# Row normalisation with each row written twice: the first load of each group as two transfers, gamma as two transfers and one broadcast

## The chip, the cores and the metric

The kernel runs on one core of one Trainium2 chip. The metric is the device time of one execution in microseconds (us). The kernel before was timed in three runs: 238.24, 238.38 and 238.87 us, so the median is 238.38. One execution was also taken with the hardware profiler. All views below are of that one.

## What is computed

```python
B, S, D = 8, 512, 2048          # x: [8, 512, 2048] float32, gamma: [2048] float32
x_rep = np.repeat(x, 2, axis=1)
rms = np.sqrt((x_rep ** 2).mean(axis=-1, keepdims=True) + 1e-6)
x_norm = x_rep / rms
return (x_norm * gamma[None, None, :]).astype(np.float32)
```

Each of the 4096 rows of x is divided by the root of its mean square, multiplied by gamma, and written twice, next to each other. So 33.55 MB are read and 67.11 MB are written.

## The kernel before

The 4096 rows go to 128 partitions in four tiles. In one tile each partition holds 8 rows that follow one another in memory, 64 KB. One large buffer `y` holds 24 rows of 2048 floats on each partition, in three regions of 8 rows: `first` (rows 0 to 7), `second` (8 to 15) and `third` (16 to 23). There are no rotating buffers: the regions are reused by hand, and the order of the instructions on each engine is the order of the program (a manual schedule). The waits between engines are put in by the framework, from who writes and reads which part of `y`.

`four(n, ...)` (L89) works on a group of two tiles, n and n+1, and is called twice. In one group:

- L92 loads the tile n to rows 4 to 11 of `y`, the upper half of `first` and the lower half of `second`. L94 loads the tile n+1 to `third`. Both are issued by SyncE (SP), one transfer each (L50).
- `squares` (L57) runs on ScalarE (ACT): for each row a Square with an accumulated sum (L63, its scratch output `sq` in PSUM), then one Sqrt for the group of rows (L67).
- `scale` (L70) runs on VectorE (DVE): the reciprocal (L73), and for each row one operation that multiplies the row by it and by gamma (L75), and writes the result to an even row of the region that is to be stored.
- `repeat` (L80) copies each even row to the odd row behind it (L82), on ACT or on DVE.
- `store` (L52) sends one region, 8 rows of each partition, to the output. There are four stores in a group, in this order: tile n's rows 0 to 3 from `first`, its rows 4 to 7 from `second`, and tile n+1's two halves from `first` again and from `third`.

The rows 0 to 3 of tile n are squared and scaled two by two, those from row 4 on four by four. All loads and stores are issued by SP, in program order: two loads, four stores, two loads, four stores. The loads of the second group write to rows that the first group's stores read, so SP waits for those stores to land before it issues them.

gamma is needed on every partition, in `gamma_b`. `constants()` (L121) is called between the two loads of the first group. ACT issues one transfer of 16 pieces of 125 floats (L122) and three of 16 floats each (L128) into rows 0 to 2 of `y` on partition 0, which the first store doesn't need yet. Then GpSimd (POOL) broadcasts first 2000 columns (L132) and then the last 48 (L136) to all partitions. A constant `eps_t` is set on DVE, and ACT takes one Sqrt of it (L140), which loads ACT's function table ahead of the work.

Of the kernel before, what the change touches and what calls it, by code (L numbers as in the profile page):

```python
# [1 line left out]

# [4 lines left out]


@with_exitstack
def kernel(  # L10
    ctx: ExitStack,
    tc: tile.TileContext,
    x: bass.AP,
    gamma: bass.AP,
    out: bass.AP,
):
    nc = tc.nc
    P = nc.NUM_PARTITIONS
    f32 = mybir.dt.float32
    Act = mybir.ActivationFunctionType  # L20
    Alu = mybir.AluOpType

    B, S, D = x.shape
    Bo, So, Do = out.shape
    R = So // S
    assert R == 2 and D == Do and B == Bo and So == S * R
    eps = 1e-6
    inv_d = 1.0 / float(D)


    K = 4
    N = B * S
    ntiles = N // (P * K)
    assert N % (P * K) == 0 and ntiles == 8
    H = 2
    x_t = x.rearrange("b s d -> (b s) d").rearrange("(n p k) d -> n p k d", p=P, k=H * K)
    out_t = out.rearrange("b s d -> (b s) d").rearrange("(n p h j) d -> n h p (j d)", p=P, h=H, j=K * R)

    singles = ctx.enter_context(tc.tile_pool(name="singles", bufs=1))
    rows = ctx.enter_context(tc.tile_pool(name="rows", bufs=1))  # L40
    junk = ctx.enter_context(tc.tile_pool(name="junk", bufs=1, space=bass.MemoryType.PSUM))
    small = ctx.enter_context(tc.tile_pool(name="small", bufs=4))

    y = rows.tile([P, 3 * K * R, D], f32, name="y")
    first, second, third = 0, K * R, 2 * K * R

    def load(n, at):
        nc.sync.dma_start(out=y[:, at : at + H * K, :], in_=x_t[n])  # L50

    def store(n, h, to):  # L52
        nc.sync.dma_start(
            out=out_t[n, h], in_=y[:, to : to + K * R, :].rearrange("p j d -> p (j d)")
        )

    def squares(at, rows):  # L57

        n = len(rows)
        ss = small.tile([P, n], f32, name=f"ss{n}")  # L60
        for c, k in enumerate(rows):
            sq = junk.tile([P, D], f32, name="sq")
            nc.scalar.activation(  # L63
                out=sq[:], in_=y[:, at + k, :], func=Act.Square, accum_out=ss[:, c : c + 1]
            )
        rms = small.tile([P, n], f32, name=f"rms{n}")
        nc.scalar.activation(out=rms[:], in_=ss[:], func=Act.Sqrt, scale=inv_d, bias=eps_t[:])  # L67
        return rms

    def scale(at, to, rows, rms):  # L70
        n = len(rows)
        rstd = small.tile([P, n], f32, name=f"rstd{n}")
        nc.vector.reciprocal(out=rstd[:], in_=rms[:])  # L73
        for c, k in enumerate(rows):
            nc.vector.scalar_tensor_tensor(  # L75
                out=y[:, to + R * k, :], in0=y[:, at + k, :], scalar=rstd[:, c : c + 1],
                in1=gamma_b[:], op0=Alu.mult, op1=Alu.mult,
            )

    def repeat(to, k0, k1, copy):  # L80
        y_r = y[:, to + R * k0 : to + R * k1, :].rearrange("p (k r) d -> p k r d", r=R)
        copy(out=y_r[:, :, 1, :], in_=y_r[:, :, 0, :])  # L82

    ctx.enter_context(tc.manual_schedule())

    half = K // 2
    up, down = list(range(K)), list(range(K - 1, -1, -1))

    def four(n, constants, step):  # L89


        load(n, first + K)  # L92
        constants()
        load(n + 1, third)  # L94
        for rows in (up[:half], up[half:]):
            scale(first + K, first, rows, squares(first + K, rows))
        repeat(first, 0, half, nc.scalar.copy)
        repeat(first, half, K, nc.vector.tensor_copy)
        store(n, 0, first)
        scale(second, second, down, squares(second, down))  # L100
        repeat(second, half, K, nc.scalar.copy)
        for k in range(0, half, step):
            repeat(second, k, k + step, nc.vector.tensor_copy)
        store(n, 1, second)
        roots = [squares(third + h * K, up) for h in range(H)]
        scale(third, first, up, roots[0])
        repeat(first, 0, half, nc.scalar.copy)
        repeat(first, half, K, nc.scalar.copy)
        store(n + 1, 0, first)
        scale(third + K, third, up, roots[1])  # L110
        repeat(third, 0, K, nc.scalar.copy)
        store(n + 1, 1, third)

    gamma_b = singles.tile([P, D], f32, name="gamma_b")
    G, E = 16, 3
    C = D // G - E
    gamma_s = y[0:1, 0:2, :].rearrange("p k (c d) -> p (k c) d", c=G // 2)
    gamma_t = y[0:1, 2, :]
    eps_t = singles.tile([P, 1], f32, name="eps_t")

    def constants():  # L121
        nc.scalar.dma_start(  # L122
            out=gamma_s[0:1, :, :C],
            in_=gamma[: G * C].rearrange("(p c d) -> p c d", p=1, c=G),
        )
        for c in range(E):
            at = G * C + c * G
            nc.scalar.dma_start(  # L128
                out=gamma_t[0:1, c * G : (c + 1) * G],
                in_=gamma[at : at + G].partition_broadcast(1),  # L130
            )
        nc.gpsimd.partition_broadcast(  # L132
            out_ap=gamma_b[:, : G * C].rearrange("p (c d) -> p c d", c=G),
            in_ap=gamma_s[0:1, :, :C],
        )
        nc.gpsimd.partition_broadcast(out_ap=gamma_b[:, G * C :], in_ap=gamma_t[0:1, : E * G])  # L136
        nc.vector.memset(eps_t, eps)  # L137

        root = singles.tile([P, 1], f32, name="root")[:]
        nc.scalar.activation(out=root, in_=eps_t[:], func=Act.Sqrt)  # L140

    four(0, constants, half)
    four(2, lambda: None, 1)


# [1 line left out]
_INS = ['x', 'gamma']  # L147
_OUTS = [((8, 1024, 2048), 'float32')]


# [23 lines left out]
```

## Time and profile before

| What | Value |
|---|---|
| median of three runs | 238.38 us (238.24 to 238.87) |
| profiled execution: its own time | 238.07 us |
| profiled execution: span from first to last instruction | 236.2 us |
| L63, Square on ACT, 32 times | 1.878 us each, 60.1 us in all |
| L75, scale on DVE, 32 times | 2.349 us each, 73.8 us in all |
| L82, copies on ACT / on DVE | 42.6 us in 10 / 9.2 us in 5 |
| first load of the first group: issued, and time to landing | 0.72 us, 21.9 us |
| first store of the first group / of the second: issued | 39.20 us / 155.30 us |

The span starts with the first instruction and ends with the last. Start times in all views are counted from it. In a view of waits, a line names an engine and a line of the program, what it waited for, the total, the number of times, and the longest. In a timeline, a line has the start, the duration, the engine, the line and the operation, and in brackets the idle time before it and what ended that. The name of an engine with a q behind it (SPq, ACTq) is its sequencer, which issues transfers. q1 is the DMA queue of SP and q10 that of ACT. Each transfer over 128 partitions is cut into packets, shared out over 16 DMA engines.

A DMA share over 1.00 in a short stretch comes about because a packet's whole time is put to the stretch in which it starts. So the share times the length of the stretch, times 16 engines, divided by the packets, is the mean time of a packet. "Packet records" are the starts and durations of single packets in the trace.

### The profile page before, as it was taken

What the parts mean: (1) busy time and instruction counts of PE and PEld (TensorE: products, weight loads), DVE (VectorE), ACT (ScalarE), POOL (GpSimd) and SP (SyncE); (2) the same over time, 40 slices, a digit from 0 to 9 for tenths busy, and PEclk for the clock granted to TensorE, in tenths of its full rate; (3) what the DMA queues carried; (4) which work ended last, traced back from release to release, by engine and by line L of the source; (5) the groups of instructions that cost most, each with busy time, mean ns of one, the idle gap of its engine ahead of it and who ended that gap; (6) DMA issues with size and microseconds to landing.
All of it is one profiled execution on the core that took longest, in us unless ns stands there. A gap on an engine that the chain in (4) does not pass through costs nothing.

```text
span 236.2 us, 226 instructions
## 1 busy us (share of the span) xinstructions
DVE 84.5 (36%) x48; ACT 110.2 (47%) x86; POOL 2.8 (1%) x6
## 2 busy tenths in 40 slices
DVE  0000396594699500000000007928919992000000
ACT  2001989479998470000000049991999957400000
POOL 0110000000000000000000000000000000000000
DMA  9898989989898989989898998989898998989894
GB/s 355 356 533 355 510 377 422 466 366 522 355 533 356 533 355 422 466 377 510 355 533 355 488 400 355 533 355 533 355 533 355 488 399 355 533 355 533 355 533 178
DMA packets 1767, 100.68 MB, mean 426 GB/s; under 512 B 230, under 2 KB 230, under 8 KB 230
## 3 DMA queue, kind: packets, MB, share of 16 engines
q1 hardware_dynamic: 1728, 100.66, 98.7%
q10 hardware_dynamic: 38, 0.01, 0.0%
q14 instruction: 1, 0.01, 0.0%
HBM read 33.56 MB, written 67.11 MB: 426 GB/s over the span
## 4 chain that ended last, share of the span: by engine, by line
DMA 45%; ACT 26%; DVE 12%; issue 2%; DVEq 0%
DMA y<-in_x_dram 26%; DMA out_dram<-y 20%; ACT sq L63 15%; DVE y L75 12%; ACT y L82 11%; ACT rms L67 1%; DVE rstd L73 0%; DVEq L75 0%
## 5 line engine op out<-in xcount | busy, mean ns | idle before, releaser
L63 ACT ACTIVATE sq<-y 128x2048 f32<-128x2048 f32 x32 | 60.1, 1878 | 71.1 <-DMA y<-in_x_dram 70.4
L75 DVE SCALAR_TENSOR_TENSOR y<-y,rstd,gamma_b 128x2048 f32<-128x2048 f32 x32 | 73.8, 2349 | 1.6 <-DMA out_dram<-y 1.0
L82 ACT COPY y<-y 128x4096 f32<-128x4096 f32 (+1 forms) x10 | 42.6, 4283 | 19.1 <-DVE y L75 18.3
L73 DVE RECIPROCAL rstd<-rms 128x4 f32<-128x4 f32 (+1 forms) x10 | 1.7, 170 | 109.2 <-ACT rms L67 109.2
L82 DVE COPY y<-y 128x4096 f32<-128x4096 f32 (+1 forms) x5 | 9.2, 1865 | 0.1
L63 ACT ACTIVATION_READ_ACCUMULATOR sq<-y 128x1 f32 x32 | 6.0, 186 | 0.0
L67 ACT ACTIVATE rms<-ss,eps_t 128x4 f32<-128x4 f32 (+1 forms) x10 | 3.0, 297 | 0.3
L140 ACT ACT_TABLE_LOAD x1 | 1.3, 1283 | 2.6 <-issue 2.6
L132 POOL PARTITION_BROADCAST gamma_b<-y x1 | 2.2, 2243 | 10.2 <-DMA y<-in_gamma_dram 10.2
L136 POOL PARTITION_BROADCAST gamma_b<-y x1 | 0.3, 323 | 10.1 <-DMA y<-in_gamma_dram 10.1
L137 DVE MEMSET eps_t<- 128x1 f32 x1 | 0.1, 59 | 0.8 <-PEq L158 0.8
L140 ACT ACTIVATE root<-eps_t 128x1 f32<-128x1 f32 x1 | 0.2, 203 | 0.0
L158 POOL MEMSET const-bfloat16-1.0<- 128x1 bf16 x1 | 0.1, 102 | 0.0
L158 POOL MEMSET const-float32-0.0<- 128x1 f32 x1 | 0.1, 99 | 0.2 <-issue 0.2
L158 POOL MEMSET const-uint8-127<- 128x1 uint8 x1 | 0.1, 101 | 0.0
L158 POOL MEMSET const-float32-1.0<- 128x1 f32 x1 | 0.1, 98 | 0.0
## 6 DMA issues: line engine op xcount, KB each, us to landing
out_dram<-y SPq DMA_DIRECT2D x8, 24.8
y<-in_x_dram SPq DMA_DIRECT2D x4, 31.4
y<-in_gamma_dram ACTq DMA_DIRECT2D x3, 0.1 KB
y<-in_gamma_dram ACTq DMA_DIRECT2D x1, 7.8 KB, 9.8
```

What stands on the lines that cost most here:

```text
L63: nc.scalar.activation(out=sq[:], in_=y[:, at + k, :], func=Act.Square, accum_out=ss[:, c : c + 1])
L67: nc.scalar.activation(out=rms[:], in_=ss[:], func=Act.Sqrt, scale=inv_d, bias=eps_t[:])
L73: nc.vector.reciprocal(out=rstd[:], in_=rms[:])
L75: nc.vector.scalar_tensor_tensor(out=y[:, to + R * k, :], in0=y[:, at + k, :], scalar=rstd[:, c : c + 1], in1=gamma_b[:], op0=Alu.mult, op ...
L82: copy(out=y_r[:, :, 1, :], in_=y_r[:, :, 0, :])
L132: nc.gpsimd.partition_broadcast(out_ap=gamma_b[:, : G * C].rearrange("p (c d) -> p c d", c=G), in_ap=gamma_s[0:1, :, :C],)
L136: nc.gpsimd.partition_broadcast(out_ap=gamma_b[:, G * C :], in_ap=gamma_t[0:1, : E * G])
L137: nc.vector.memset(eps_t, eps)
L140: nc.scalar.activation(out=root, in_=eps_t[:], func=Act.Sqrt)
L158: nc = _bacc.Bacc("TRN2", target_bir_lowering=False, num_devices=1)
```

## The change

Two parts. The first load of each group, in `four`, is issued as two transfers: rows 0 to 3 of each partition, then rows 4 to 7. The second load of a group stays one transfer. And gamma goes straight to partition 0 of `gamma_b`, in two transfers of 16 pieces of 64 floats (each takes one half of each stretch of 128 floats), and one broadcast of all 2048 columns from partition 0 of `gamma_b` to `gamma_b`. Rows 0 to 2 of `y` are no longer used for gamma.

```diff
-    def load(n, at):
-        nc.sync.dma_start(out=y[:, at : at + H * K, :], in_=x_t[n])
+    def load(n, at, parts=1):
+        w = H * K // parts
+        for k in range(0, H * K, w):
+            nc.sync.dma_start(out=y[:, at + k : at + k + w, :], in_=x_t[n][:, k : k + w, :])
...
-        load(n, first + K)
+        load(n, first + K, H)
         constants()
         load(n + 1, third)
...
-    G, E = 16, 3
-    C = D // G - E
-    gamma_s = y[0:1, 0:2, :].rearrange("p k (c d) -> p (k c) d", c=G // 2)
-    gamma_t = y[0:1, 2, :]
...
-        nc.scalar.dma_start(
-            out=gamma_s[0:1, :, :C],
-            in_=gamma[: G * C].rearrange("(p c d) -> p c d", p=1, c=G),
-        )
-        for c in range(E):
-            at = G * C + c * G
-            nc.scalar.dma_start(
-                out=gamma_t[0:1, c * G : (c + 1) * G],
-                in_=gamma[at : at + G].partition_broadcast(1),
-            )
-        nc.gpsimd.partition_broadcast(
-            out_ap=gamma_b[:, : G * C].rearrange("p (c d) -> p c d", c=G),
-            in_ap=gamma_s[0:1, :, :C],
-        )
-        nc.gpsimd.partition_broadcast(out_ap=gamma_b[:, G * C :], in_ap=gamma_t[0:1, : E * G])
+        G, E = 16, 2
+        w = D // G // E
+        g_in = gamma.rearrange("(p c d) -> p c d", p=1, c=G)
+        g_to = gamma_b[0:1, :].rearrange("p (c d) -> p c d", c=G)
+        for c in range(0, D // G, w):
+            nc.scalar.dma_start(out=g_to[:, :, c : c + w], in_=g_in[:, :, c : c + w])
+        nc.gpsimd.partition_broadcast(out_ap=gamma_b[:], in_ap=gamma_b[0:1, :])
         nc.vector.memset(eps_t, eps)
```

## The prediction

> **What bounds the kernel now.** I read the page's busy shares, then the DMA queues, then the share of the DMA engines in stretches of time, then the waits, and last the timeline around the two loads that the change splits.
>
> ```profile
> DVE 84.5 (36%) x48; ACT 110.2 (47%) x86; POOL 2.8 (1%) x6
> ...
> q1 hardware_dynamic: 1728, 100.66, 98.7%
> q10 hardware_dynamic: 38, 0.01, 0.0%
> ```
>
> No compute engine is busy for half of the span, while the 16 DMA engines spend 98.7% of it on q1, the queue of the x loads and the stores. What matters is where the missing 1.3% lies. Here are three stretches (start:end, length, busy time of DVE, ACT and POOL, clock, DMA share, GB/s):
>
> ```profile
> 0.00:1.70 1.70, 0.06 (x1) 0.00 (x0) 0.19 (x4) 1.00 0.00 0
> 1.70:235.05 233.35, 84.44 (x47) 110.16 (x86) 2.57 (x2) 1.00 1.00 431
> 235.05:236.20 1.15, 0.00 (x0) 0.00 (x0) 0.00 (x0) 1.00 0.00 0
> ```
>
> Between 1.70 and 235.05 the share is 1.00. The idle time is 1.70 us before the first packet (the first load is issued at 0.72 us) and 1.15 us after the last. So the transfers alone set the end, and a change can move it only by (a) making the transfers take more or less engine time, (b) moving the first packet or the tail, or (c) opening a hole in the stream.
>
> The waits seem to say something else:
>
> ```profile
> ACT sq L63 <- DMA y<-in_x_dram: 70.4, 2, 51.8
> ...
> SPq L53 <- DVE y L82: 84.1, 4, 35.2
> SPq L53 <- ACT y L82: 60.9, 4, 19.9
> ```
>
> ScalarE waits 70.4 us for loads, and the store queue waits for compute. But while those queues wait, the DMA engines work off what was issued before. The place to check is where loads run out and the first store must follow:
>
> ```profile
> 22.67 1.88 ACT L63 ACTIVATE sq<-y 128x2048 f32<-128x2048 f32 x1 [18.58 <-DMA y<-in_x_dram]
> ...
> 39.20 48.22 SPq L53 DMA_DIRECT2D out_dram<-y  x4
> ...
> 155.30 48.29 SPq L53 DMA_DIRECT2D out_dram<-y  x4
> ```
>
> Squares start at 22.67, when the whole first load has landed, and the first store is issued at 39.20. The DMA queue view for 36 to 46 us has q1 at 99.9%, so the loads reach past 41 us and the store follows without a hole. From issue to first packet the first load took 1.70-0.72 = 0.98 us, so the store was ready at about 40.2, some 0.8 us before the first engine came free at about 41.0 (packet records). In the second half it is ready at 156.3, against 157.3. The cover is thin but it holds.
>
> **The change, part by part.**
>
> *The first load of each group in two halves.* 100.66 MB in 12 transfers is 8.39 MB each, 19.5 us at 431 GB/s. A half lands 9.7 us earlier, so squares start near 13.0 instead of 22.67 and the store's chain, 39.20-22.67 = 16.5 us long, issues it near 29.5. What that saves is nothing: at 29.5 the engines still hold 11.5 us of loads, and the store waits behind them in its queue. The second group is alike: its first load, issued at 100.04, waits for the third store's landing as before, and the fourth store, in flight until about 119, hides that wait and SP's extra issue (0.36 us, from the row of L50). Later stores don't move the end either; the third needs a buffer that the first store frees near 61 us, whatever was computed before.
>
> What the halves add on the engines: 128 packets of 64 KB become 256 of 32 KB, 8 more on each engine, and one completion packet, per split load. The trace has no 32 KB packet, so I bound one packet's fixed part by the small ones, the two phases of the large gamma transfer on q10:
>
> ```profile
> q1 hardware_dynamic: 16, 1.05, 242.3%
> q10 hardware_dynamic: 16, 0.01, 2.6%
> ...
> ```
> ```profile
> q1 hardware_dynamic: 16, 1.05, 302.3%
> q10 hardware_dynamic: 16, 0.00, 1.1%
> ...
> ```
>
> The first pair is the stretch 7 to 8 us: 16 pieces of 500 B took 2.6% of 16 engine-us, 0.026 us each. The second is 9.5 to 10.3: 16 completion packets took 1.1% of 12.8, 0.009 us each, beside 64 KB packets of 302.3% x 12.8 / 16 = 2.418 us, or 27.1 B/ns. The 500 B at that rate are 0.018 us, which leaves 0.008 as the fixed part. Low end: nothing (bytes alone count; a gain is excluded, since the bytes stay and packets are only added). High end: the whole 0.026 for each added packet. I take 0.008, because a 32 KB packet streams as the large ones do. Sum for two loads: 2 x (8 x 0.008 + 0.009) = 0.15 us; high end 2 x (8 x 0.026 + 0.009) = 0.43 us. None of it is hidden, since the engines have no spare time.
>
> The rule that speaks against the split is in the Trainium skill, DMA: Bandwidth & Descriptors, "Anatomy of one DMA": a transfer costs a constant of about 2.0 us beside its bytes (fitted for transfers that GpSimd issues). By it, two added loads would make an estimated 238.07+4.0 = 242.1 us. The row of 36 to 46 us disagrees for queued transfers: one transfer ends and the next begins within it, and 99.9% of the engines' time is taken.
>
> *Gamma.* ACT issues two transfers instead of four (0.59 and 1.21 us of issue in the trace, in the 18 us in which ACT has nothing to square). On the engines, each had 0.026+0.009, and one had three small pairs more; now each has two pairs, at most 0.070 in all. The difference is below 0.04 us either way and I take 0. A wait could matter: the first scale now needs both transfers and a broadcast of all 2048 columns about 9.7 us sooner, at 27.34-9.7 = 17.6.
>
> ```profile
> 10.65 2.24 POOL L132 PARTITION_BROADCAST gamma_b<-y  x1 [10.22 <-DMA y<-in_gamma_dram]
> ...
> 23.01 0.32 POOL L136 PARTITION_BROADCAST gamma_b<-y  x1 [10.12 <-DMA y<-in_gamma_dram]
> ```
>
> Each q10 packet waits for one x packet of its engine: pieces at 7 to 8, completions at 9.5 to 10.3, and the three small pairs, six more turns, until 23.0. In the changed kernel the second transfer needs two turns more: 10.3 + 2 x 2.45 = 15.2, and the broadcast 2.24 x 2048/2000 = 2.3, so 17.5 at the latest; turns behind 32 KB packets are half as long, which gives nearer 10. If gamma came as late as 23.0, the broadcast would end at 25.3, DVE and the copies and store queued behind it would slip 7.7 us to 37.2, and that is still before 40. So cost 0, hidden by the loads; beyond 10.5 us of delay it would cost microsecond for microsecond. POOL has nothing else to do.
>
> *The new order of waits.* In the compiled order, SP's second store waits for the second half-load too, landed by 22, and the second half-load of group two also waits for the second store, landed near 80 before the 100 at which it is issued. Nothing behind them is late.
>
> *Sum.* The profiled execution: 238.07 (1.70 + 233.35 + 1.15, and 1.87 around the span) + 0.15 = 238.22. It lies 0.31 under the median of the three runs, 238.38, so for a median I forecast 238.38 + 0.15 = **238.5 us**.
>
> **Rivals.**
>
> *Slower: each added load opens the stream anew.* The queue view of 1.7 to 2.3 us has 16 packets with 537.3% of 16 x 0.6 engine-us, 3.22 us each, 0.81 over the usual 2.418. If a transfer of half the size pays that opening, two do: 238.5 + 1.6 = 240.1. It decides (over 0.72 us) from 0.28 us a load on, next to the 0.15. Against it: the boundaries between transfers in the trace show no such packets. For it: no row shows 32 KB packets or two loads from interleaved rows.
>
> *Faster: the thin cover had holes, or the stream's slow packets go.* The timed median is 0.31 over the profiled run and the slowest 0.80; if that were holes before the stores, 10 us of cover would close them: 238.07+0.15 = 238.2, still no change by my bound, and from the slowest run's level at best -0.65. To gain more, the opening's 0.81 and the slow packets near 116 us (323.4% x 12.8 / 16 = 2.59 each in 115.8 to 116.6, 0.17 over) must go as well: 238.2-1.0 = 237.2. Nothing in the change touches what makes them.
>
> *Compute was the bound after all.* If the 9.7 us by which compute moves forward reached the end in both groups, the time would be 238.4-19.4 = 219.0. A share of 1.00 over 233.35 us excludes it.
>
> *The halves don't land apart.* If the two half-loads ran interleaved, squares would start near 22 as now, and the time would be the same 238.5. Against it: the same queue's transfers land one after another, 19.3 us apart.
>
> **How the numbers follow.** A measurement of this kernel tells a change from none at about 0.3%, 0.72 us: the three runs spread over 0.63. No change 0.71 (the forecast with its costs, and the halves that don't land apart); slower 0.19 (the opening of loads, and other fixed costs above 0.04 us a packet); faster 0.10, nearly all of it the holes and slow packets, as the compute rival has next to nothing. The range: up to the slowest of the three runs plus the high end, 238.87+0.43 = 239.3; down to 237.7, the point where the faster case begins, which leaves out about a tenth on either side.
>
> **What would show it.** Right: squares start near 13, the first store is issued near 29.5 and lands, as before, near 61; q1 has 1728 + 2 x 144 = 2016 packets and a share of 1.00 from the first packet to the last; a stretch in the first load shows 32 KB packets of about 1.21 us. Wrong: those packets above 1.25 us, a stretch with a share under 1.00 at 12, 41, 129 or 158 us, or a first packet later than 1.7 us.

## The result and the profile after

The changed kernel takes 239.62 us (median of 6 runs, 239.31 to 239.96), the kernel before in the same comparison 238.39 us (238.24 to 238.87). The ratio is 1.0049, with a 95% interval of 1.0036 to 1.0062. So it is slower by 1.2 us, above the range of the prediction.

The profiled execution took 239.46 us, with a span of 237.6, against 238.07 and 236.2 before. What lies around the span is unchanged (1.86 and 1.87 us). The stretches of time of the changed kernel, cut where the first packet starts and the last ends (columns as in the prediction):

```profile
0.00:1.70 1.70, 0.06 (x1) 0.00 (x0) 0.19 (x4) 1.00 0.00 0
1.70:236.45 234.75, 84.44 (x47) 110.66 (x86) 2.29 (x1) 1.00 1.00 429
236.45:237.60 1.15, 0.00 (x0) 0.00 (x0) 0.00 (x0) 1.00 0.00 0
```

Start and tail are the same. The stream is still without a hole, but it is 1.40 us longer for the same bytes: 234.75 against 233.35. Packets took longer somewhere.

The plan of the work is what the prediction says. Lines of the timeline of the changed kernel:

```profile
10.80 2.29 POOL L126 PARTITION_BROADCAST gamma_b<-gamma_b  x1 [10.38 <-DMA gamma_b<-in_gamma_dram]
13.09 1.88 ACT L65 ACTIVATE sq<-y 128x2048 f32<-128x2048 f32 x1 [9.60 <-DMA y<-in_x_dram]
...
29.62 59.10 SPq L55 DMA_DIRECT2D out_dram<-y  x4
```

Squares start at 13.09 instead of 22.67, gamma is ready at 13.1, and the first store is issued at 29.62 instead of 39.20. What becomes of the ten microseconds is seen in the waits of the changed kernel:

```profile
ACT sq L65 <- DMA y<-in_x_dram: 52.1, 3, 42.0
...
DVE y L77 <- DMA out_dram<-y: 21.3, 2, 10.8
```

The second line in the kernel before, where it is L75:

```profile
DVE y L75 <- DMA out_dram<-y: 1.0, 2, 0.6
```

ScalarE waits 18 us less for loads (70.4 before), and VectorE waits 20 us more for stores to land. The work is done earlier and then waits for the DMA engines.

Now the queue q1 in the stretch from 38.5 to 39.2 us, in which the 16 DMA engines start the last packets of the two loads (one of them starts just behind it in the kernel before). First the kernel before, then the changed one (columns: packets, MB, share of the 16 engines):

```profile
DMA packets 15, 0.98 MB, mean 1404 GB/s; under 512 B 0, under 2 KB 0, under 8 KB 0
...
q1 hardware_dynamic: 15, 0.98, 324.8%
```
```profile
DMA packets 16, 1.05 MB, mean 1498 GB/s; under 512 B 0, under 2 KB 0, under 8 KB 0
...
q1 hardware_dynamic: 16, 1.05, 538.9%
```

A share times the stretch, times 16, divided by the packets, is the time of one packet: 3.248 x 0.7 x 16 / 15 = 2.43 us before, and 5.389 x 0.7 = 3.77 us after. Each engine's last load packet takes longer, by 1.35 us on average, with the same 64 KB, and with no idle time around it. It is the largest part of the 1.40 us. What differs at that moment is that in the changed kernel the store has stood in the same queue for nine microseconds, while before it was issued at 39.20, when these packets had just started. The same place in the second group doesn't show it, though the store is as early there (issued at 146.84; stretch 155.8 to 156.6 of the changed kernel):

```profile
q1 hardware_dynamic: 15, 0.98, 287.6%
...
```

That is 2.876 x 0.8 x 16 / 15 = 2.45 us a packet.

The packets of half the size fit the prediction's price. Sixteen packets of the second half-load (stretch 13 to 14 us of the changed kernel):

```profile
q1 hardware_dynamic: 16, 0.52, 121.3%
...
```

A 32 KB packet takes 1.213 us, 0.004 over half of 2.418, so 0.008 for each pair, as priced.

### The profile page after: what moved, and what is told of

Read it like the earlier page. It is cut to its first block, busy times and chain, and to the rows that moved or that the text cites. A ratio compares the mean times of both kernels' runs of the same rounds, so it can differ in the third digit from the quotient of the medians.

```text
span 237.6 us, 221 instructions
## 1 busy us (share of the span) xinstructions
DVE 84.5 (36%) x48; ACT 110.7 (47%) x86; POOL 2.5 (1%) x5
## 4 chain that ended last, share of the span: by engine, by line
DMA 56%; DVE 15%; ACT 14%; issue 1%; DVEq 0%; SPq 0%
DMA out_dram<-y 38%; DMA y<-in_x_dram 17%; DVE y L77 15%; ACT y L84 8%; ACT sq L65 6%; ACT rms L69 0%; DVE rstd L75 0%; DVEq L77 0%; SPq L52 0%
## 5 line engine op out<-in xcount | busy, mean ns | idle before, releaser
L75 DVE RECIPROCAL rstd<-rms 128x4 f32<-128x4 f32 (+1 forms) x10 | 1.7, 170 | 90.3 <-ACT rms L69 90.3
L126 POOL PARTITION_BROADCAST gamma_b<-gamma_b x1 | 2.3, 2292 | 10.4 <-DMA gamma_b<-in_gamma_dram 10.4
```

The lines of the kernel that those rows point to most:

```text
L126: nc.gpsimd.partition_broadcast(out_ap=gamma_b[:], in_ap=gamma_b[0:1, :])
```

## The experiments

Theory A: a store that stands in the queue when the loads end makes the last load packets longer. Its rivals are named as they come up. In the diffs, lines of the kernel before start with a minus, unless another kernel is named.

**One part of the change at a time.** `e1` is the changed kernel with unsplit loads:

```diff
-        load(n, first + K, H)
+        load(n, first + K)
```

> The changed gamma (two transfers of 16 pieces, one broadcast), loads not split. Theory A (the added time is made where the first group's loads give way to its first store, because that store is queued ten microseconds early): no early store here, so 238.4 us, and the last packets of the second load, which start near 38.6 us, take 2.42 us as before. Theory B (the new gamma transfers cost the time): 239.5 us. Theory C (each added load has its own cost): 238.4 us.

`e2` and `e3` are the kernel before with the changed kernel's `load`, called with two parts in the first group alone, or in the second alone:

```diff
-        load(n, first + K)
+        load(n, first + K, H if n == 0 else 1)      # e2; e3: n == 2
```

> Only the first group's first load in two halves, gamma as before. Theory A: 238.4 + 0.07 (half of the packets' cost) + about 1.1 = 239.6 us, with packets of some 3.8 us from 38.6 us on. Theory B: 238.5 us. Theory C: half of the whole, 239.0 us.

> Only the second group's first load in two halves, gamma as before. Theory A, as the profile of the changed kernel has it (the change from loads to stores in the second group cost 0.1 us): 238.6 us. If an early store costs as much in any group, only not in that one execution: 239.6 us. Theory B: 238.5 us. Theory C: 239.0 us.

`e9`, run later, splits both and leaves gamma as before.

> Both first loads in two halves, gamma as before. If the cost comes once in an execution, at the first change from loads to stores that finds its store queued: 239.5 us, 0.1 us above the first group's split alone. If both groups pay as they do when split alone (1.1 and 1.0 us): 240.4 us. If the new gamma carries part of the whole change's 1.23 us: 239.0 us or less.

| Kernel | Time, us | Before beside it | Ratio, 95% interval |
|---|---|---|---|
| e1, gamma only | 238.82 | 238.24 | 1.0013 to 1.0042 |
| e2, first group split | 239.36 | 238.24 | 1.0031 to 1.0057 |
| e3, second group split | 239.24 | 238.24 | 1.0021 to 1.0052 |
| e9, both split, old gamma | 239.57 | 238.33 | 1.0034 to 1.0063 |

The split alone costs what the whole change costs: e9 adds 1.24 us, the whole change 1.23. So theory B, that the new gamma carries it, falls. Theory C, a cost of each added load, falls too: one split costs as much as two. Each group alone pays about a microsecond, and together they don't pay two. The last load packets ahead of the first store, in e2 (38.5 to 39.1 us) and e3 (second group, 154.9 to 155.7 us):

```profile
q1 hardware_dynamic: 16, 1.05, 591.2%
...
```
```profile
q1 hardware_dynamic: 16, 1.05, 410.4%
...
```

They take 5.912 x 0.6 = 3.55 us and 4.104 x 0.8 = 3.28 us. So the second group can pay it too, if the first has not. In e9, as in the whole change, the first group's packets take 3.67 us and the second's are near 2.5. In all of these runs the cost comes once, at the first change from loads to stores that finds its store already queued.

**Gamma alone has a cost that the whole change doesn't have.** e1 is 0.58 us slower than before, where I expected nothing. In its profile the last load packets take 2.42 us. The stream ends 0.25 us later (by packet records that is one late engine; on average the engines end no later than before), and 0.34 us more lie outside the span (238.80 - 236.6 = 2.2 against 1.87). The whole change shows none of that (1.86), and e9 0.1 us of it (239.58 - 237.6 = 2.0). The records had a fetch of instructions by one DMA engine that moved from 75 us to 152 us. `e6` brings it back by making ScalarE's program longer where it idles:

```diff
-        nc.scalar.activation(out=root, in_=eps_t[:], func=Act.Sqrt)
+        for _ in range(16):
+            nc.scalar.activation(out=root, in_=eps_t[:], func=Act.Sqrt)
```

(from e1)

> The gamma-only kernel with 15 more of the one-element Sqrts of the constants at the start of ScalarE's stream, where it idles until 22 us. Theory F (what gamma cost is a fetch of instructions by one DMA engine, which moved from 75 us to 152 us into the loads because ScalarE's program became shorter, and there costs the last engine 0.3 us): the fetch moves back, 238.3 us. Rival G (the gamma transfers themselves, wherever the fetch lies): 238.8 us.

The fetch did move back to 75 us, and the time stayed at 238.85 us (before: 238.18). So theory F falls. Again 2.2 us lie outside the span. Why gamma alone lengthens what lies around the span is open. In the whole change it has no share, since nothing is added around the span there.

**Hold the early store back.** In `e4` (the whole change) and `e5` (e2) the first store waits for one element that GpSimd copies late:

```diff
-        store(n, 0, first)
         scale(second, second, down, squares(second, down))
+        late = small.tile([P, 1], f32, name="late")
+        nc.gpsimd.tensor_copy(out=late[:], in_=y[:, second + R * (K - 2), 0:1])     # e5: K - 1
+        nc.gpsimd.tensor_copy(out=y[:, first + 7, 0:1], in_=y[:, first + 6, 0:1])
+        store(n, 0, first)
```

(in the first group; the element has the value that is there already)

> The whole change, but the first group's first store is held back by two tiny GpSimd copies that follow the second scaled row of the next four: issued at about 39.4 us instead of 29.6 us, all the work on ScalarE and VectorE where it was. Theory A: 238.6 us, the packets from 38.6 us on at 2.42 us again. A rival D (the copies and scales that now run at 39 to 43 us slow the last packets of the load): 239.6 us, as the changed kernel. Theories B and C: 239.6 us.

> Only the first group's first load in two halves, gamma as before, and the first store held by two tiny GpSimd copies behind the first scaled row of the next four: issued near 39.1 us, just in time, as in the kernel before. Theory A (a store that stands in the queue when the last packets of the loads begin makes those packets longer): 238.3 us, and the packets from 38.6 us on take 2.42 us. Rival E (the half-loads do it in some other way, and the early store only happens beside it): 239.4 us, as without the hold.

Both missed their moment. One of the two copies took 2.2 us, beside VectorE's scaling. In e4 the store was issued at 41.45, after the loads had ended. A hole of 1.1 us followed, and later changes cost more as well, so the kernel took 241.44 us. The last load packets of the first group (38.4 to 39.2 us) and of the second (156.8 to 157.6 us):

```profile
q1 hardware_dynamic: 16, 1.05, 302.3%
...
```
```profile
q1 hardware_dynamic: 16, 1.05, 419.6%
...
```

In the first group they take 3.023 x 0.8 = 2.42 us, beside the same copies and scales as in the changed kernel, so rival D falls. In the second group, where the store is early (147.52), they take 3.36 us: as in e3, the second group pays when the first has not. And the packets at the change from stores to loads (16 that start from 117.4 to 117.6 us, with a share of 1581.0%) take 3.16 us. e5's store came at 39.53, 0.3 later than in the kernel before. Its last load packets are normal too, but it took 239.96 us, more than rival E forecast. Most of the time was lost at the change from stores to loads (packets of up to 3.6 us around 116 and 119 us).

`e7`, `e8` and `n1` (all from e2) hold the first group's first store with ScalarE instead:

```diff
-        store(n, 0, first)
-        scale(second, second, down, squares(second, down))
+        root2 = squares(second, down)
+        for _ in range(2):                       # e8: none
+            sq = junk.tile([P, D], f32, name="sq")
+            nc.scalar.activation(out=sq[:], in_=y[:, second, :], func=Act.Square)
+        # n1: one more Square, of 950 columns; e7: a copy of one element
+        nc.scalar.copy(out=y[:, first + 7, 0:1], in_=y[:, first + 6, 0:1])
+        store(n, 0, first)
+        scale(second, second, down, root2)
```

> Only the first group's first load in two halves, gamma as before; the first store waits for one element that ScalarE copies after two spare squares, so it is issued near 39.1 us, 0.1 us before the kernel before issues it and 0.4 us before the held store that came out at 240.0 us. Theory K (the change from loads to stores is free when the store comes just before the last load packet ends, and costs 1.1 us when it stands in the queue earlier): 238.3 us, every packet from 38.6 us to 41 us at 2.42 us. Rival L (split loads lose the microsecond somewhere in any case, at the first change or at the later one): 239.4 us or more.

> The same without the two spare squares: the first store is issued near 34.8 us, five microseconds later than with the split alone, but two packets before the loads end. Theory K, with only the last packet of the loads counting: 239.4 us, as with the split alone. If the cost goes by how long the store has stood in the queue: about 238.8 us.

> The first group's first load in two halves, gamma as before, and the first store issued at 39.2 us, where the kernel before issues it (two spare squares and one of 950 columns on ScalarE ahead of the element that it waits for). Theory K: 238.3 us, packets from 38.6 us at 2.42 us but for a tenth or so. Rival L: 239.0 us or more, the cost found at the first change or at the later one.

With them the size of the cost can be set against the moment at which the store is issued. The last load packets start at 38.4 to 39.2 us and end, if nothing lengthens them, at 40.9 to 41.6:

| First store issued at | Kernel | Last load packet, us | Time, us |
|---|---|---|---|
| 29.56 | e2 | 3.55 | 239.36 |
| 34.50 | e8 | 3.75 | 239.40 |
| 38.31 | e7 | 3.21 | 238.98 |
| 39.23 | n1 | 2.42 | 239.91 |
| 39.20 | before | 2.43 | 238.18 to 238.39 |

The rows for e8 (38.6 to 39.2 us) and e7 (38.4 to 39.1 us) rest on these lines:

```profile
q1 hardware_dynamic: 16, 1.05, 624.9%
...
```
```profile
q1 hardware_dynamic: 16, 1.05, 457.9%
...
```

Five microseconds more or less ahead of the end make no difference (e2, e8). A store issued 0.1 to 0.7 us before the last packets start costs part of it (e7). One issued when they have just started (0.2 to 0.7 us before, in n1) costs nothing there. So at the first change it is the early store that costs, not the split load. Lines of the view of n1 from 38.4 to 39.1 us:

```profile
DMA packets 16, 1.05 MB, mean 1498 GB/s; under 512 B 0, under 2 KB 0, under 8 KB 0
...
q1 hardware_dynamic: 16, 1.05, 346.1%
```

3.461 x 0.7 = 2.42 us. But n1 as a whole did not come back to 238.3. Two of its nine runs took 238.43 and 238.55 us, the other seven 239.66 to 240.31. In the profiled one (240.06) single engines fall behind at the change from stores to loads, the second group's first load lands with its slowest engine, squares start at 140.64 instead of 138.85, and the store that had come at 155.30 comes at 157.09: a hole of 0.39 us on average over the engines. One engine stays behind to the end: it finishes at 236.88 us, where 14 of the 16 are done by 235.61 (packet records). What makes engines fall behind there is open. The two runs near 238.5 speak against rival L in its strict form, a loss in any case, but for the usual run it is not excluded.

**The cost by itself, with no computation.** `m2` and `m3` keep only the transfers: the stores send a region that VectorE sets to a constant.

```python
nc.vector.memset(y[:, third : third + H * K, :], 0.5)
for what in "LLLLSSSSSSSS":               # m3: "LSSLSSLSSLSS"
    load to first or second in turn, or store from third
```

> No computation at all: the four loads, then the eight stores of a constant region, everything queued as early as its buffers allow, so one change from loads to stores. Theory A with one cost of about 1.1 us for each such change: about 236 us (231.9 of packets, 0.8 of the opening, 1.1 of one change, 1.7 ahead of the first packet), and the last packets of the fourth load long. Rival H (nothing but a queue that stands full, no change needed): long packets elsewhere too.

> The same twelve transfers without computation, in the order load, store, store, four times over, so four changes from loads to stores and three back. Theory A with a cost for each change from loads to stores: 3 x 1.1 = 3.3 us over the kernel with one change, more if the way back costs too. Rival I (the cost comes once in an execution, at the first such change): the same time as with one change.

`m4` and `n2` are m2 with the constant written in more pieces, so that the stores are issued late.

> The kernel with one change and no computation, with the constant region written in six pieces, so that the stores are issued near 78 us, just before the four loads end, instead of 42 us. Theory K: 1.0 us less than with the stores queued at 42 us, 238.2 us, and the packets from 77.4 us on take 2.42 us. Rival M (the change costs the same whenever the stores are queued): 239.2 us.

> No computation, four loads and eight stores, the stores issued near 78.0 us. Theory K: 238.1 us, 1.1 us less than with the stores queued at 42 us, the packets from 77.4 us at 2.42 us and no hole behind them. Rival M: 239.2 us.

| Kernel | Stores issued from | Last load packets, us | Time, us |
|---|---|---|---|
| m2 | 42.30 | 3.47 | 239.22 (238.97 to 239.34) |
| n2 | 77.93 | 2.45 | 238.12 (237.90 to 238.56) |
| m4 | 93.24 | 2.42 | 252.41, a hole of 14.3 us |
| m3, four changes to stores | 17.95 | 3.58 at the first, 2.64 at the second | 240.53 (239.97 to 240.92) |

The packets from 77.3 to 78.0 us, in m2 and then in n2:

```profile
q1 hardware_dynamic: 16, 1.05, 496.0%
...
```
```profile
q1 hardware_dynamic: 16, 1.05, 349.8%
...
```

The same twelve transfers in the same order, with no computation and no split load, take 1.1 us less when the stores are issued just after the last load packets have started (77.31 to 77.81 us). Rival M falls, and so does rival H: no other packets are long in m2 but the first ones, which open the stream (by up to 1.03 us), and these. (m4's pieces were written more slowly than I had reckoned; it says no more than that its load packets, with no store behind them, are normal. The 236 us expected of m2 left out the end of the span and what lies around it, 1.3 and 1.8 us.) m3 shows the cost at the first change to stores, 3.58 us a packet, then 2.64 and less: rival I is right about the large part. The later changes to stores add 0.12 to 0.22 us each. That is less than half of the 1.3 us by which m3 is above m2. Most of the rest is one engine that ends late, at 237.40 us against 236.64 for the next (packet records).

**The change back, from stores to loads.** In the kernel before, the second group's first load stands in the queue from 100 us, and the last packets of the fourth store, near 116 us, take 2.59 us. `n3` holds that load with sixteen spare squares of ScalarE:

```diff
+        if n != 0:
+            for c in [D] * 15 + [1700]:
+                sq = junk.tile([P, D], f32, name="sq")
+                nc.scalar.activation(out=sq[:, :c], in_=gamma_b[:, :c], func=Act.Square)
+            nc.scalar.copy(out=y[:, second + K - 1, 0:1], in_=eps_t[:])
         load(n, first + K)
```

> The kernel before, with the second group's first load held by spare squares on ScalarE until 116.7 us instead of 100.0 us, so that it comes just before the fourth store ends. Theory K, if it holds for the change from stores to loads too: the packets near 116 us go from 2.59 us on average to 2.42 us, and the time falls by 0.2 us to about 238.1 us, within what can be told from no change. If that change is free of it: 238.3 us. If the load comes late: a hole, and more than 238.5 us.

It took 238.89 us (before 238.33; ratio 1.0017 to 1.0039). The load was issued at 117.45, somewhat late. The store's last packets are normal now, but the load's first packets are not (stretch 118.4 to 119.1 of n3):

```profile
q1 hardware_dynamic: 31, 1.05, 445.9%
...
```

With 16 data packets and 15 tiny ones that is 4.459 x 0.7 = 3.12 us each, as at the start of the kernel (3.22). So here a load that comes just in time pays its opening, 0.7 us, where the same kernel with the load queued early pays 0.17. But early is not always cheap in this direction: with the load queued some 16 us ahead, the packets in front of it cost nothing in the changed kernel, 0.17 us in the kernel before and 0.74 in e4 (3.16 against 2.42). No version that computes came out ahead of the kernel before.

## Why the prediction was wrong, point by point

- **What bounds the kernel: right.** The DMA share is 1.00 from the first packet to the last in both kernels, and the time follows the stream's length: 1.40 us in the profiled runs. The signs listed for "wrong" (slow small packets, a hole, a later start) did not come; a longer last packet of the loads was not on the list.
- **The ten microseconds save nothing: right.** Squares at 13.09 (13.0 forecast), the first store at 29.62 (29.5). They turned into waits of VectorE for stores.
- **The packets of half the size: right.** 1.213 us each; 8 x 0.008 + 0.009 for each load, as priced.
- **Gamma: right for the whole change.** e9 without it takes 239.57 us, the whole change 239.62. For gamma alone the cost 0 was wrong: e1 is 0.58 us slower, and why is open.
- **The step that failed** is the sentence "What that saves is nothing: at 29.5 the engines still hold 11.5 us of loads, and the store waits behind them in its queue." It takes a transfer that waits in a queue to be without effect on the one ahead of it. The store made the last packet of the loads longer on every engine, by 1.35 us on average (3.77 against 2.43). I had asked of the early store only whether it could close a hole, and so gave "early" no price at all, neither in the sum nor in the upper end of the range.
- **What the profile of before had shown.** It has both cases. At 41 and 157 us the change from loads to stores is free, and there the store is issued 1.8 and 2.0 us before the first engine comes free. Near 116 us, where loads had stood queued for 15 us behind the store, packets took 2.59 instead of 2.42 us. I read those as slow packets that "nothing in the change touches"; they lie at the one change of direction with an early successor. That row gave the sign, but not the size: a price of 0.17 us would still have been about eight times too low. The free change in the second group of the kernel before, from 154.8 to 155.6 us (3.025 x 0.8 = 2.42 us):

```profile
q1 hardware_dynamic: 16, 1.05, 302.5%
...
```
- **The thin cover.** The lead of 0.98 us from issue to first packet was about right: engines that had run dry got their first store packet 0.84 us after the issue (e4 and m4), and e5's second store, issued 0.87 us before the first engine came free, left at most 0.05 us on an engine. But e5's first store, issued 1.5 us ahead, had packets start 0.05 us late on average, and why is open.
- **The slower rival** had the right sign and nearly the right price (0.81 for each added load), but the wrong place and mechanism: no load opens the stream anew (after the first, each 32 KB packet takes 1.213 us), and one split load costs as much as two.
- **The sum, put right:** 0.15 for the packets, 1.35 at the first change to stores, 0.04 at the second, less the 0.17 that the kernel before pays near 116 us and the changed one doesn't, and less 0.20 at the opening. The first packets take 0.81 us over the usual 2.418 before, and 2.271 x 0.8 = 1.82 us after (1.7 to 2.5 us), 0.60 over the usual 1.213:

```profile
q1 hardware_dynamic: 16, 0.52, 227.1%
...
```

That makes 1.17 us. By packet records the engines end 1.14 us later on average (235.96 against 234.81). The stream is 1.40 us longer because its end is that of the slowest engine, which is 0.46 us behind the average in the changed kernel and 0.19 before. The medians differ by 1.23.

What is not settled is why the cost comes only once at the changes to stores, and what decides the cost of the way back, which lay between 0 and 0.74 us with the load queued early. The runs show that for the cost at the change to stores the store must already be queued when the last load packets start, and that these packets are stretched. Between two transfers of the same direction, queued one behind the other, packets are normal (m2). What the engine does in that time, no view shows.

## What to carry to other kernels

In a kernel whose DMA engines never idle, finishing work earlier saves nothing, and it can cost: when a store enters the queue is itself part of the change, and the place to price it is the packets ahead of the change of direction. Before calling a moved transfer free, look in the profile for a place where its like already stands queued, and read the time of the packets in front of it: it can give the sign, though here not the size. A margin of 1.8 us that looks thin can be just what is wanted. And a stream ends with its slowest engine, so a sum of mean packet times is to be held against the mean end, not the last.

## What the runs showed of the hardware that was not expected

- A store queued before the last load packets start lengthens each engine's last load packet of 64 KB from 2.42 us to between 3.2 and 3.8 us, at the first such change of an execution; later such changes cost 0.22 us or less (m3, e9, the changed kernel).
- A load that follows stores just in time paid 0.7 us on each engine's first packet (n3); queued some 16 us ahead, the store in front of it paid nothing (the changed kernel), 0.17 us (the kernel before) or 0.74 us (e4).
- A store issued 1.6 to 2.0 us before the first engine comes free followed without a hole (n1, the kernel before, e1); 1.5 us ahead its first packets were 0.05 us late on average (e5's first), 0.87 us ahead at most 0.05 us on an engine (e5's second), and 0.5 us after it there was a hole of 1.1 us (e4).
- The fixed part of a packet is small beside all this: 32 KB take 1.213 us and 64 KB take 2.418.
